# Experts' transposes taken in pairs of blocks, one-hots in the second pair, gathered tokens in one group, and a small tile of norms in another pool

## The chip, the cores and the metric

The kernel runs on one core of a Trainium2 chip. The time is device microseconds of that core, the median of the runs shown.

## What is computed

A decoder trunk of two layers over 256 tokens of width 1024: causal pooling and a dense SwiGLU, then attention over shared keys and values and a layer of eight experts of which each token takes two. The change lies in the experts, whose reference, cut, is:

```python
logits = (xf @ w_router).astype(jnp.float32)
top_val, top_idx = lax.top_k(logits, TOP_K)      # TOP_K = 2
gates = jax.nn.softmax(top_val, axis=-1)
# tokens sorted by expert, each expert's block runs that expert only
h = jax.nn.silu(xb @ w_gate[e]) * (xb @ w_up[e])  # 1024 -> 3584
y_block = h @ w_down[e]                           # 3584 -> 1024
y = jnp.zeros((T, D)).at[tok_s].add(g_s[:, None] * ys[dest])
```

## The kernel before

An expert takes up to 128 tokens at once. Its 3584 inner units are cut into seven blocks of 512 (`hidden_block(b)`, b = 0 to 6). A block is eight steps of gate and up (`ps_mg`, then `ps_mu`), and, from block 2 on, four steps of the down product of the block two before (`ps_y`); the down products of the last two blocks, eight steps, close the expert, so it has 84 steps. A step takes a weight tile of 128x1024 numbers (half of a 1 MB load), splits it into a high part (`wh`, ScalarE, L180) and a low part (`wl`, VectorE, L184), and runs six TensorE matmuls of 512 columns: four with `wh` (L192), two with `wl` (L195). Activations are split the same way (`xeH`/`xeL`, `hid`), so every product is three matmuls.

The order is written by hand. `run()` walks the steps; before a step's matmuls are written down, the splits up to three steps ahead are, and after it `tick()` runs what `later(n, fn)` has put off by n steps. Each engine keeps this order. SyncE fetches weights into a ring of 11 slots of 1 MB, each slot fetched again when its `wl` has been made.

Between the steps TensorE has smaller work, all through the four PSUM banks of `bankB`:

- `turn_hidden(hs, b)`: four transposes of the block's 128x512 inner units (`ps_hT`, L1113), four steps after the block is done; then ScalarE and VectorE write `hid` from PSUM (L1121, L1122). Seven such groups in an expert.
- `seek(e + 1)`, begun six steps into block 2: VectorE writes the next expert's one-hots (L1073); two steps later `find` transposes them (two transposes, L1079), ScalarE copies the result to `ohT` (L1080), and two small products (four passes, L1025) give, in the same PSUM bank, the row numbers of that expert's tokens, which VectorE casts into `src` (L1026); four steps after that GpSimd issues the indirect DMA (L1029) that fetches those rows into `xm`.
- `gather(slots, q, name)`: the fetched tokens are transposed in two groups of four (`ps_x`, L1060) and split into `xeH`/`xeL`; 5 and 8 steps after the last block.
- `scatter`: the expert's output is added to the tokens (L1127 to L1130).

The first expert, expert 0, has more: it takes its tokens by a product (L1064), and the gates of all experts (L987 to L998) and the tokens' store (`ship`, L1011) fall into its first blocks.

`rstds`, 48 numbers per partition of reciprocal norms, lies in the pool `cst`; a filler of 16 numbers lies in `resid`, one of `PHASE_FILL` bytes in `mp`. The pools are laid out one behind the other, so these sizes set the addresses of what follows.

Of the kernel before, what the change touches and what calls it, by code (L numbers as in the profile page):

```python
# [12 lines left out]
F32 = mybir.dt.float32  # L13
# [15 lines left out]
TL = 3  # L29
# [9 lines left out]
TURN = 4  # L39
P = 128  # L40
T = 256
# [4 lines left out]
FE = 3584  # L46
NB = FE // 512
LAG = 2
PHASE_FILL = 160
EPS = 1e-6  # L50
NEG = -1e30
WINDOWS = (2, 4, 8, 16)
# [45 lines left out]
def trunk(ctx, tc, x, a_norm, a_proj, a_scale, kv_norm, w_kv, b_norm, w_q, w_o, rel_bias,  # L98
          ffn_norm, w_gate, w_up, w_down, moe_router, moe_gate, moe_up, moe_down, final_norm,
          c_misc, c_band, c_onehot, c_mask, out):  # L100
    nc = tc.nc
# [5 lines left out]
    cst = ctx.enter_context(tc.tile_pool(name="cst", bufs=1))  # L107
# [4 lines left out]
    resid = ctx.enter_context(tc.tile_pool(name="resid", bufs=1))  # L112
# [23 lines left out]
    def later(n, fn, rank=1):  # L136
        serial[0] += 1
        pending.append((clock[0] + n, rank, serial[0], fn))
# [133 lines left out]
    nc.vector.memset(ones, 1.0)  # L272
    mhalf = cst.tile([P, 2], F32, name="mhalf")
    nc.vector.memset(mhalf, -0.5)
    rstds = cst.tile([P, 48], F32, name="rstds")
    taken = []


# [41 lines left out]
        return ap.rearrange("p (m i r) -> p m i r", i=2, r=2)  # L320

    h2 = resid.tile([P, 2, D], F32, name="h2")
    resid.tile([P, 16], F32, name="fill")
    sq = h2.rearrange("p i (k t) -> p (i k) t", t=T)

    hT_ctx, hp = phase("hp", side="right")
# [483 lines left out]
    mo = {}  # L810
# [5 lines left out]
    def last_merge():  # L816
# [23 lines left out]
        mo["src"] = mp.tile([P, NE], I32, name="src")  # L840
        mp.tile([P, PHASE_FILL // 4], F32, name="fill")
        spare = av["big"][:, 4096:]
# [162 lines left out]
    got = []  # L1005
    rows = dpool.tile([T, D], F32, name="rows")

    def ship():
# [6 lines left out]
        nc.vector.tensor_copy(tok[:, 0:1], pn[:, :1])  # L1015
        nc.vector.tensor_scalar(tok[:, 1:2], pn[:, :1], float(P), None, op0=ALU.add)

    def seek(e):
        plain = plain_onehots(e, mo["pos"], "")

        def find():
            ohT = mo["ohT", e] = mo["m1"].tile([P, 2, P], F32R, tag=f"ohT{e % 2}", name=f"ohT{e}")
            po = turn_onehots(e, plain, ohT, "")
            for i in range(2):
                nc.tensor.matmul(po[:, T:T + 1], plain[:, i, :], mo["tok"][:, i:i + 1], start=(i == 0), stop=(i == 1))  # L1025
            nc.vector.tensor_copy(mo["src"][:, e:e + 1], po[:, T:T + 1])  # L1026

        later(2, find)
        later(6, lambda: nc.gpsimd.indirect_dma_start(  # L1029
            out=mo["xm"][:, e % 2, :], out_offset=None, in_=rows,  # L1030
            in_offset=bass.IndirectOffsetOnAxis(ap=mo["src"][:, e:e + 1], axis=0)))

    then(route)

# [38 lines left out]
            nc.vector.tensor_scalar(plain[:, i, :], iota, slot[:, i, e:e + 1], None, op0=ALU.is_equal)  # L1073
        return plain

    def turn_onehots(e, plain, ohT, sfx):
        po = bankB(f"ps_oh{sfx}{e}")
        for i in range(2):
            nc.tensor.transpose(po[:, i * P:(i + 1) * P], plain[:, i, :], ident)  # L1079
        nc.scalar.activation(ohT.rearrange("p i t -> p (i t)"), po[:, :T], AF.Copy)  # L1080
        return po

# [21 lines left out]
    def expert(e, got, sfx, next_expert=None):  # L1104
# [2 lines left out]
        hidden = [None] * NB  # L1107
        full = (NB - 1,) if next_expert is None else ()

        def turn_hidden(hs, b):  # L1110
            pt = bankB(f"ps_hT{sfx}{e}_{b}")
            for c in range(4):
                nc.tensor.transpose(pt[:, c * P:(c + 1) * P], hs[:, c * P:(c + 1) * P], ident)  # L1113
            ptv = pt.rearrange("p (c s) -> p c s", c=4)
            if b in full:
                hidden[b] = mo["m1"].tile([P, NK, P], F32, tag="xeH", name=f"hid{sfx}{e}_{b}")[:, :4, :]
                nc.scalar.activation(hidden[b], ptv, AF.Copy)
                return
            both = mo["m1"].tile([P, 4, 2, P], F32R, tag="hid", name=f"hid{sfx}{e}_{b}", bufs=3)
            hidden[b] = (both[:, :, 0, :], both[:, :, 1, :])  # L1120
            nc.scalar.activation(hidden[b][0], ptv, AF.Copy)  # L1121
            nc.vector.tensor_sub(hidden[b][1], ptv, hidden[b][0].bitcast(F32))  # L1122
# [13 lines left out]
        def hidden_block(b):  # L1136
            nm = f"{sfx}{e}_{b}"
            ps = {}

            def acc(w):  # L1140
                def f():
                    if w not in ps:
                        ps[w] = bankA(f"ps_m{w}{nm}")
                    return ps[w]
                return f

            def gate_done():
                hs = ps["h"] = mo["m1"].tile([P, 512], F32, tag=f"hs{b % 2}", name=f"hs{nm}")
                nc.scalar.activation(hs, ps["g"], AF.Silu)

            def up_done():
                nc.vector.tensor_mul(ps["h"], ps["h"], ps["u"])
                later(TL if b == NB - 1 and next_expert is None else TURN, lambda: turn_hidden(ps["h"], b))

            for w, src, fn in (("g", moe_gate, gate_done), ("u", moe_up, up_done)):
                for kh in range(2):
                    moe_unit(src[e, kh * 512:(kh + 1) * 512, b * 512:(b + 1) * 512], acc(w),
                             lambda: (got()[1], got()[2]), 4 * kh, kh == 0, kh == 1, f"m{w}{nm}_{kh}",
                             fn if kh == 1 else None)
# [57 lines left out]
    for e in range(NE):  # L1217
        def next_expert(e=e):
            got.append(new_slots(e + 1, ""))
            for q in range(2):  # L1220
                later(5 + 3 * q, lambda q=q: gather(got[e + 1], q, f"{e + 1}_{q}"))

        expert(e, lambda e=e: got[e], "", next_expert if e + 1 < NE else None)
    with tc.manual_schedule():
# [72 lines left out]
```

## Time and profile before

| | us |
|---|---|
| median of 3 runs | 1515.49 (1515.38 to 1523.37) |
| the profiled execution, device time | 1520.44 |
| its span, first to last instruction | 1518.6 |
| TensorE busy in the span | 1488.2 (98%) |
| experts, first step to last product (526.1 to 1505.2) | 979 |

Matmuls are pipelined and the profile models their ends, so they overlap in it: two matmuls of 512 columns that each show 0.39 us start 0.227 us apart. Where TensorE has no gap, the distance from one start to the next is what an instruction costs.

### The profile page before, as it was taken

How to read it: one execution, taken by the hardware profiler on the slowest of the kernel's cores; microseconds unless marked ns; L12 is line 12 of the kernel's file. 1: busy time of each engine (PE TensorE's matmuls, PEld its weight loads, DVE VectorE, ACT ScalarE, POOL GpSimd, SP SyncE). 2: the span in 40 equal slices, each digit the busy share in tenths (PEclk: the TensorE clock that was granted, in tenths of full speed). 3: DMA queues.
4: the chain of work that ended last, by engine and by line, in shares of the span. 5: the costliest groups of instructions: out<-in, count | busy, mean ns of one | idle time of the engine just before them, and what ended most of it. 6: DMA issues, size and time to landing. Idle time of an engine off the chain costs nothing. (4 is left out here: it accounts for less than half of the span.)

```text
span 1518.6 us, 22313 instructions
## 1 busy us (share of the span) xinstructions
PE 1488.2 (98%) x8711; PEld 1300.2 (86%) x8711; DVE 1191.5 (78%) x1341; ACT 1007.2 (66%) x1208; POOL 19.8 (1%) x23
## 2 busy tenths in 40 slices
PE   8999999999999999999999999999999999999996
PEld 7999999999999978888888888888888888888884
DVE  6666556464545588999999899999899899899984
ACT  5444445444444577777777777777777777777773
POOL 0000000000000000000000000000000000000001
PEclk9999999999999999999999999999999999999998
DMA  9955684737464799999999999999999999999931
GB/s 307 313 181 177 192 211 158 201 127 186 139 174 139 281 364 383 374 349 371 366 357 376 376 353 365 378 364 357 370 375 354 374 377 351 368 364 362 371 127 30
DMA packets 276083, 445.79 MB, mean 294 GB/s; under 512 B 28848, under 2 KB 100784, under 8 KB 275968
## 3 DMA queue, kind: packets, MB, share of 16 engines
q1 hardware_dynamic: 252448, 433.11, 80.8%
q10 hardware_dynamic: 22512, 7.50, 3.2%
q0 software_dynamic: 1008, 3.67, 0.6%
q8 instruction: 70, 1.15, 0.3%
q14 instruction: 45, 0.37, 0.1%
HBM read 442.03 MB, written 2.22 MB: 293 GB/s over the span
## 5 line engine op out<-in xcount | busy, mean ns | idle before, releaser
L184 DVE TENSOR_TENSOR wl_mu<-raw_mu,wh_mu 128x1024 fp32r<-128x1024 f32 x196 | 232.1, 1219 | 36.2 <-ACT wh_mu L180 36.2
L184 DVE TENSOR_TENSOR wl_mg<-raw_mg,wh_mg 128x1024 fp32r<-128x1024 f32 x204 | 243.1, 1220 | 15.4 <-ACT wh_mg L180 14.0
L192 PE MATMUL ps_y<-wh_md,hid 128*128 128x512 f32 x880 | 238.2, 392 | 0.0
L180 ACT ACTIVATE wh_mg<-raw_mg 128x1024 fp32r<-128x1024 f32 x204 | 213.5, 1060 | 36.8 <-PE ps_y L192 28.7
L184 DVE TENSOR_TENSOR wl_md<-raw_md,wh_md 128x1024 fp32r<-128x1024 f32 x190 | 223.0, 1219 | 1.5 <-ACT wh_md L180 1.5
L180 ACT ACTIVATE wh_mu<-raw_mu 128x1024 fp32r<-128x1024 f32 x196 | 203.5, 1057 | 20.3 <-PE ps_mg L192 20.2
L180 ACT ACTIVATE wh_md<-raw_md 128x1024 fp32r<-128x1024 f32 x190 | 195.4, 1057 | 22.7 <-PE ps_mu L192 13.6
L192 PEld LDWEIGHTS ps_y<-wh_md,hid 128*128 128x128 f32 x880 | 163.6, 188 | 33.4 <-issue 0.5
L192 PE MATMUL ps_mg<-wh_mg,xeH 128*128 128x512 f32 x448 | 178.6, 399 | 0.0
L192 PE MATMUL ps_mu<-wh_mu,xeH 128*128 128x512 f32 x448 | 176.1, 393 | 0.0
L192 PE MATMUL ps_mg<-wh_mg,xeL 128*128 128x512 f32 x448 | 174.8, 390 | 0.0
L192 PE MATMUL ps_mu<-wh_mu,xeL 128*128 128x512 f32 x448 | 174.5, 389 | 0.0
L195 PE MATMUL ps_mu<-wl_mu,xeH 128*128 128x512 f32 x448 | 138.2, 390 | 1.1 <-DVE wl_mu L184 1.1
L195 PE MATMUL ps_mg<-wl_mg,xeH 128*128 128x512 f32 x448 | 138.3, 390 | 0.0
L195 PE MATMUL ps_y<-wl_md,hid 128*128 128x512 f32 x440 | 135.7, 390 | 0.0
L195 PEld LDWEIGHTS ps_mu<-wl_mu,xeH 128*128 128x128 f32 x448 | 84.0, 188 | 19.3 <-DVE wl_mu L184 1.6
L195 PEld LDWEIGHTS ps_mg<-wl_mg,xeH 128*128 128x128 f32 x448 | 83.9, 188 | 18.5 <-DVE wl_mg L184 0.2
L192 PEld LDWEIGHTS ps_mu<-wh_mu,xeL 128*128 128x128 f32 x448 | 84.2, 188 | 17.0
L192 PEld LDWEIGHTS ps_mu<-wh_mu,xeH 128*128 128x128 f32 x448 | 84.1, 188 | 17.0
L192 PEld LDWEIGHTS ps_mg<-wh_mg,xeL 128*128 128x128 f32 x448 | 84.3, 188 | 16.4
L192 PEld LDWEIGHTS ps_mg<-wh_mg,xeH 128*128 128x128 f32 x448 | 84.2, 188 | 16.3
L195 PEld LDWEIGHTS ps_y<-wl_md,hid 128*128 128x128 f32 x440 | 82.6, 188 | 17.6
(255 smaller groups left out, 2644.5 us busy)
## 6 DMA issues: line engine op xcount, KB each, us to landing
raw_mg<-in_moe_w_gate_dram SPq DMA_DIRECT2D x102, 1024.0 KB, 7.0
raw_mu<-in_moe_w_up_dram SPq DMA_DIRECT2D x98, 1024.0 KB, 7.2
raw_md<-in_moe_w_down_dram SPq DMA_DIRECT2D x96, 1024.0 KB, 6.9
big<-in_moe_w_down_dram SPq DMA_DIRECT2D x16, 1024.0 KB, 7.4
big<-in_moe_w_up_dram SPq DMA_DIRECT2D x14, 1024.0 KB, 6.6
raw_k<-in_w_kv_dram SPq DMA_DIRECT2D x12, 1024.0 KB, 5.3
raw_q<-in_w_q_dram SPq DMA_DIRECT2D x12, 1024.0 KB, 5.5
raw_v<-in_w_kv_dram SPq DMA_DIRECT2D x12, 1024.0 KB, 5.3
```

The costliest lines, as they stand in the source:

```text
L180: nc.scalar.activation(hv, raw, AF.Copy)
L184: nc.vector.tensor_sub(lv, raw, hv.bitcast(F32))
L192: nc.tensor.matmul(o, a, b, start=start and k == 0 and m == 0, stop=False)
L195: nc.tensor.matmul(o, a, b, start=False, stop=stop and k == n - 1)
```

## The change

Three things move and one tile changes its place. Inner units: a done block is put on a list, `waiting`; the list is transposed four steps after blocks 1, 3, 5 and 6, so blocks 0 and 1, 2 and 3, 4 and 5 go together. One-hots: `find` is put on a list, `riders`, which is emptied with the next such group (that of blocks 2 and 3), and its two small products now stand ahead of ScalarE's copy. Tokens: both groups of four are put off by 2 steps. `rstds` goes from `cst` to `resid`, the filler there goes, `PHASE_FILL` is 96: the weight ring, `wh` and `wl` lie 192 bytes lower, the tiles of `xp`, `aqp` and `bigp` 64 lower, those of `mp` and `m1` 64 higher (all shifts are multiples of 64 bytes).

```diff
-PHASE_FILL = 160
+PHASE_FILL = 96
-    rstds = cst.tile([P, 48], F32, name="rstds")
+    rstds = resid.tile([P, 48], F32, name="rstds")
-    resid.tile([P, 16], F32, name="fill")
...
+    riders = []
     def seek(e):
         plain = plain_onehots(e, mo["pos"], "")
         def find():
             ohT = mo["ohT", e] = mo["m1"].tile([P, 2, P], F32R, tag=f"ohT{e % 2}", name=f"ohT{e}")
-            po = turn_onehots(e, plain, ohT, "")
-            for i in range(2):
-                nc.tensor.matmul(po[:, T:T + 1], plain[:, i, :], mo["tok"][:, i:i + 1], start=(i == 0), stop=(i == 1))
+            po = turn_onehots(e, plain, ohT, "", mo["tok"])
             nc.vector.tensor_copy(mo["src"][:, e:e + 1], po[:, T:T + 1])
-        later(2, find)
-        later(6, lambda: nc.gpsimd.indirect_dma_start(
+        riders.append(find)
+        riders.append(lambda: later(3, lambda: nc.gpsimd.indirect_dma_start(
...
+    def turn_onehots(e, plain, ohT, sfx, tok=None):
         po = bankB(f"ps_oh{sfx}{e}")
         for i in range(2):
             nc.tensor.transpose(po[:, i * P:(i + 1) * P], plain[:, i, :], ident)
+        if tok is not None:
+            for i in range(2):
+                nc.tensor.matmul(po[:, T:T + 1], plain[:, i, :], tok[:, i:i + 1], start=(i == 0), stop=(i == 1))
         nc.scalar.activation(ohT.rearrange("p i t -> p (i t)"), po[:, :T], AF.Copy)
...
+        waiting = []
+        def turn_waiting():
+            pts = [(b, turn_hidden(hs, b)) for hs, b in waiting]
+            waiting.clear()
+            while riders:
+                riders.pop(0)()
+            for b, pt in pts:
+                keep_hidden(pt, b)
         def turn_hidden(hs, b):
             pt = bankB(f"ps_hT{sfx}{e}_{b}")
             for c in range(4):
                 nc.tensor.transpose(pt[:, c * P:(c + 1) * P], hs[:, c * P:(c + 1) * P], ident)
+            return pt
+        def keep_hidden(pt, b):
...
-                later(TL if b == NB - 1 and next_expert is None else TURN, lambda: turn_hidden(ps["h"], b))
+                waiting.append((ps["h"], b))
+                if b % 2 or b == NB - 1:
+                    later(TL if b == NB - 1 and next_expert is None else TURN, turn_waiting)
...
-                later(5 + 3 * q, lambda q=q: gather(got[e + 1], q, f"{e + 1}_{q}"))
+                later(2, lambda q=q: gather(got[e + 1], q, f"{e + 1}_{q}"))
```

On TensorE, expert 2, before: the one-hots of expert 3, behind block 2 (its last step's `wl` rows first), with the semaphores that each row waits for.

```order
L195 MATMUL ps_mu_2_8190<-wl_mu_2_1_1_8187,xeH_7812 128x512 [waits DVE_49]
L195 MATMUL ps_mu_2_8190<-wl_mu_2_1_1_8187,xeH_7812 128x512
L1079 MATMUL ps_oh_8234<-misc,oh_8208 128x128 [waits DVE_49] x2
L1025 MATMUL ps_oh_8234<-tok,oh_8208 128x1 [waits Activation_49]
L1025 MATMUL ps_oh_8234<-tok,oh_8208 128x1
L192 MATMUL ps_y_0_8246<-wh_md_0_0_0_8198,hid_0_8081 128x512 x4
```

And in the change, behind the down product of block 1:

```order
L195 MATMUL ps_y_1_8260<-wl_md_1_1_1_8373,hid_1_8180 128x512 [waits DVE_49]
L195 MATMUL ps_y_1_8260<-wl_md_1_1_1_8373,hid_1_8180 128x512
L1125 MATMUL ps_hT_2_8416<-misc,hs_2_8183 128x128 x4
L1125 MATMUL ps_hT_3_8421<-misc,hs_3_8324 128x128 x4
L1078 MATMUL ps_oh_8427<-misc,oh_8207 128x128 [waits PE_49]
L1078 MATMUL ps_oh_8427<-misc,oh_8207 128x128
L1081 MATMUL ps_oh_8427<-tok,oh_8207 128x1 x2
L192 MATMUL ps_mg_4_8444<-wh_mg_4_0_0_8384,xeH_7811 128x512 [waits Activation_49]
```

The small products have lost their wait for ScalarE; the one-hots wait only for TensorE's own earlier use of the bank, blocks 2 and 3 stand together, and the group that stood alone behind block 2 is gone.

On VectorE, expert 0, before, from the last of the gates to the down product of block 0:

```order
L998 SCALAR_TENSOR_TENSOR gat<-sel,gv_5769,gat 128x8
L1122 TENSOR_TENSOR hid_1_6058<-ps_hT_1_6053,hid_1_6058 128x4x128
L184 TENSOR_TENSOR wl_mu_2_1_1_6064<-big_5483,wh_mu_2_1_1_6063 128x1024
L184 TENSOR_TENSOR wl_md_0_0_0_6075<-raw_md_0_0_5550,wh_md_0_0_0_6074 128x1024
L1073 TENSOR_SCALAR oh_6084<-misc,pos 128x128 x2
L184 TENSOR_TENSOR wl_md_0_0_1_6088<-raw_md_0_0_5550,wh_md_0_0_1_6087 128x1024
L184 TENSOR_TENSOR wl_md_1_0_0_6100<-raw_md_1_0_6097,wh_md_1_0_0_6099 128x1024
L1026 CAST src<-ps_oh_6110 128x1
L1152 TENSOR_TENSOR hs_2_6061<-hs_2_6061,ps_mu_2_6067 128x512
L184 TENSOR_TENSOR wl_md_1_0_1_6119<-raw_md_1_0_6097,wh_md_1_0_1_6118 128x1024
```

And in the change:

```order
L997 SCALAR_TENSOR_TENSOR gat<-sel,gv_5768,gat 128x8
L1137 TENSOR_TENSOR hid_0_6054<-ps_hT_0_6044,hid_0_6054 128x4x128
L1137 TENSOR_TENSOR hid_1_6057<-ps_hT_1_6049,hid_1_6057 128x4x128
L184 TENSOR_TENSOR wl_mu_2_1_1_6063<-big_5482,wh_mu_2_1_1_6062 128x1024
L184 TENSOR_TENSOR wl_md_0_0_0_6074<-raw_md_0_0_5549,wh_md_0_0_0_6073 128x1024
L1072 TENSOR_SCALAR oh_6083<-misc,pos 128x128 x2
L184 TENSOR_TENSOR wl_md_0_0_1_6087<-raw_md_0_0_5549,wh_md_0_0_1_6086 128x1024
L184 TENSOR_TENSOR wl_md_1_0_0_6099<-raw_md_1_0_6096,wh_md_1_0_0_6098 128x1024
L1167 TENSOR_TENSOR hs_2_6060<-hs_2_6060,ps_mu_2_6066 128x512
L184 TENSOR_TENSOR wl_md_1_0_1_6110<-raw_md_1_0_6096,wh_md_1_0_1_6109 128x1024
```

`hid_0`, which stood six weight splits earlier, now stands right ahead of `hid_1` and of the last split of block 2; the cast of `src` has gone to the group of blocks 2 and 3.

## Rows read from the trace of the kernel before

**Rows 1.** Page, part 1: busy us, share of the span, instructions.

```profile
PE 1488.2 (98%) x8711; PEld 1300.2 (86%) x8711; DVE 1191.5 (78%) x1341; ACT 1007.2 (66%) x1208; POOL 19.8 (1%) x23
```

**Rows 2.** One expert: stretch, length, busy us by engine, PEclk, DMA share, GB/s.

```profile
782.30:904.20 121.90, 121.43 (x556) 100.28 (x555) 111.52 (x110) 94.93 (x103) 0.94 (x1) 1.00 1.01 367
```

**Rows 3.** Timeline of PE, one group: start, us, line, count [idle before <-releaser].

```profile
602.30 1.07 PE L192 MATMUL ps_y<-wh_md,hid 128*128 128x512 f32 x4
...
603.67 0.60 PE L1113 MATMUL ps_hT<-misc,hs 128*128 128x128 f32 x4
...
606.87 0.39 PE L192 MATMUL ps_mg<-wh_mg,xeH 128*128 128x512 f32 x1
...
608.23 0.39 PE L192 MATMUL ps_mg<-wh_mg,xeH 128*128 128x512 f32 x1
```

**Rows 4.** Timeline of PE, expert 0: two groups that already stand together.

```profile
554.57 0.51 PE L985 MATMUL ps_count<-both,ones 128*128 128x8 f32 x4
554.93 0.63 PE L1113 MATMUL ps_hT<-misc,hs 128*128 128x128 f32 x4
...
559.52 0.39 PE L192 MATMUL ps_mu<-wh_mu,xeH 128*128 128x512 f32 x1
```

**Rows 5.** Timeline of PE, expert 2: the one-hots for expert 3.

```profile
806.93 0.38 PE L1079 MATMUL ps_oh<-misc,oh 128*128 128x128 f32 x2
807.79 0.61 PE L1025 MATMUL ps_oh<-tok,oh 128*128 128x1 f32 x4 [0.47 <-ACT ohT L1080]
808.25 1.17 PE L192 MATMUL ps_y<-wh_md,hid 128*128 128x512 f32 x4
...
811.08 1.07 PE L192 MATMUL ps_y<-wh_md,hid 128*128 128x512 f32 x4
```

**Rows 6.** Waits: engine, line <- waited for: us in total, times, longest.

```profile
PEld ps_oh L1025 <- ACT ohT L1080: 4.9, 7, 0.7
```

**Rows 7.** Timeline of PE, expert 0: the end of block 2 and its one-hots.

```profile
561.72 0.74 PE L195 MATMUL ps_mu<-wl_mu,xeH 128*128 128x512 f32 x2 [1.13 <-DVE wl_mu L184]
563.05 0.52 PE L1079 MATMUL ps_oh<-misc,oh 128*128 128x128 f32 x2 [0.60 <-DVE oh L1073]
...
564.52 1.16 PE L192 MATMUL ps_y<-wh_md,hid 128*128 128x512 f32 x4
```

**Rows 8.** Timeline of DVE in the same place and ahead of it.

```profile
549.86 2.36 DVE L184 TENSOR_TENSOR wl_mg<-raw_mg,wh_mg 128x1024 fp32r<-128x1024 f32 x2 [2.10 <-ACT wh_mg L180]
...
561.58 1.22 DVE L184 TENSOR_TENSOR wl_md<-raw_md,wh_md 128x1024 fp32r<-128x1024 f32 x1
...
563.11 2.35 DVE L184 TENSOR_TENSOR wl_md<-raw_md,wh_md 128x1024 fp32r<-128x1024 f32 x2
...
566.04 1.22 DVE L184 TENSOR_TENSOR wl_md<-raw_md,wh_md 128x1024 fp32r<-128x1024 f32 x1
```

**Rows 9.** Timeline of ACT, expert 0: block 0's `hid`.

```profile
543.19 0.60 ACT L1121 ACTIVATE hid<-ps_hT 128x512 fp32r<-128x512 f32 x1 [1.19 <-PE ps_hT L1113]
543.69 0.59 ACT L1149 ACTIVATE hs<-ps_mg 128x512 f32<-128x512 f32 x1
```

**Rows 10.** Timeline of ACT behind the group of Rows 3.

```profile
604.80 1.05 ACT L180 ACTIVATE wh_mg<-big 128x1024 fp32r<-128x1024 f32 x1
```

**Rows 11.** Timeline of DVE behind the same group.

```profile
605.88 1.23 DVE L184 TENSOR_TENSOR wl_mg<-big,wh_mg 128x1024 fp32r<-128x1024 f32 x1 [0.26 <-ACT wh_mg L180]
```

**Rows 12.** Groups of DVE, 777 to 900 us: busy us, mean ns | idle before.

```profile
L184 DVE TENSOR_TENSOR wl_mu<-raw_mu,wh_mu 128x1024 fp32r<-128x1024 f32 x23 | 27.3, 1217 | 3.3 <-ACT wh_mu L180 3.3
L184 DVE TENSOR_TENSOR wl_mu<-big,wh_mu 128x1024 fp32r<-128x1024 f32 x6 | 7.2, 1220 | 1.6 <-ACT wh_mu L180 1.6
```

**Rows 13.** Timeline of POOL, 800 to 900 us.

```profile
809.07 0.94 POOL L1029 DMA_INDIRECT xm<-rows,src  x1 [120.94 <-DVE src L1026]
```

**Rows 14.** The same line's instructions: time from issue to landing.

```profile
DMA to landing us min/median/max: 5.7/7.9/8.3
```

**Rows 15.** Waits of SyncE's queue.

```profile
SPq L165 <- DVE wl_mg L184: 303.8, 107, 18.8
```

More of the change, by code (lines that the diff above doesn't have):

```diff
@@ L1022, in find @@
             ohT = mo["ohT", e] = mo["m1"].tile([P, 2, P], F32R, tag=f"ohT{e % 2}", name=f"ohT{e}")
-            po = turn_onehots(e, plain, ohT, "")
-            for i in range(2):
-                nc.tensor.matmul(po[:, T:T + 1], plain[:, i, :], mo["tok"][:, i:i + 1], start=(i == 0), stop=(i == 1))
+            po = turn_onehots(e, plain, ohT, "", mo["tok"])
             nc.vector.tensor_copy(mo["src"][:, e:e + 1], po[:, T:T + 1])
-        later(2, find)
-        later(6, lambda: nc.gpsimd.indirect_dma_start(
+        riders.append(find)
+        riders.append(lambda: later(3, lambda: nc.gpsimd.indirect_dma_start(
             out=mo["xm"][:, e % 2, :], out_offset=None, in_=rows,
-            in_offset=bass.IndirectOffsetOnAxis(ap=mo["src"][:, e:e + 1], axis=0)))
+            in_offset=bass.IndirectOffsetOnAxis(ap=mo["src"][:, e:e + 1], axis=0))))
     then(route)
@@ L1074, in plain_onehots @@
         return plain
-    def turn_onehots(e, plain, ohT, sfx):
+    def turn_onehots(e, plain, ohT, sfx, tok=None):
         po = bankB(f"ps_oh{sfx}{e}")
```

## The prediction

> **What bounds the kernel now.** I read the page's busy shares first, then the stretches of single experts, then TensorE's timeline around each small group, and last the waits. TensorE is busy for 98% of the span [rows 1], and in a middle expert for 121.43 of 121.90 us at a granted clock of 1.00, the 2.4 GHz level, while VectorE has 111.52 and ScalarE 94.93 us of work [rows 2]. Busy time alone would not prove a bound, so look at starts: a step of six matmuls follows the last after 1.36 us (606.87 to 608.23 [rows 3]), and 84 such steps are 114.2 of the 121.9 us. The rest is TensorE's small groups, and each moves all that follows by its own length. So in the experts a TensorE wait or switch that goes is time that goes. Weights are not late: SyncE's queue waits for `wl` to free a slot [rows 15], not for memory.
>
> The Trainium skill (Perfetto Trace Analysis, Identifying the Most-Contended Engine) says that matmul busy time is a poor measure of TensorE and that weight-load busy time should be taken. By it TensorE stands at 86% [rows 1] with a seventh of its time to spare, and the sum below would be 0; the even 1.36 us of the steps speaks against that reading here, and it is the third rival below.
>
> **What a switch costs.** From the first of four transposes to the step start two steps behind the next is 606.87 - 603.67 = 3.20 us; two steps are 2.72, so the group costs 0.48. Inside, four take 0.60 us with a last one of 0.27 (their usual length), so one follows the other after 0.11, and four are 0.44 at most (0.435 by finer reading). The switch to transposes and back is therefore about 0.05 [rows 3]. One place shows two groups already together, four count passes and four transposes: from 554.57 to 559.52 are 4.95 us for both and three steps (4.08), so 0.87 [rows 4]; with 0.48 for the transposes the four passes cost 0.39 there, 0.09 less than a group alone. I take 0.05, being the same kind of instruction, and keep 0.03 to 0.09.
>
> *Pairs of blocks.* Three groups fewer in each of eight experts, 24 x 0.05 = 1.2 us. *Tokens in one group:* seven experts, 7 x 0.05 = 0.35. Together 1.55 (0.9 to 2.8), all on TensorE's path.
>
> *One-hots, experts 1 to 6.* The group costs 811.08 - 806.93 - 2.72 = 1.43 us [rows 5], of which most is a stop: the small products wait for ScalarE to copy the transposes out of the bank, 0.7 us seven times [rows 6]. In the change they precede the copy and have no such wait. What is left is two transposes at 0.11 and four passes at (808.25 - 807.79) / 4 = 0.115: 0.68 (0.60 to 0.80), with no switch of its own. Saved 0.75 each, 6 x 0.75 = 4.5 us (3.8 to 5.0).
>
> *One-hots, expert 0.* VectorE is behind here: the last `wl` of block 2 comes 1.13 us late, then the transposes wait 0.60 for VectorE's one-hots, then the products for ScalarE [rows 7]. Block 2 ends at 561.72 + 2 x 0.227 = 562.17; the down product starts at 564.52: 2.35 us, of which 0.68 comes back later, so 1.67. The cover: the down steps now start at 562.17 and ask for their `wl` 0.91 us into each, at 563.08, 564.44, 565.80 and 567.16. VectorE delivers at 562.80 (561.58 + 1.22), 564.33 (563.11 + 1.22), 565.46, and, without the cast of 0.15 ahead of it, 567.11 [rows 8]. All four are in time, the last by 0.05. This is the thinnest cover of the change.
>
> *Block 0's `hid` in expert 0.* It goes from ScalarE's place at 543.19, where ScalarE had waited 1.19 us for the transposes and 0.50 passes before the next instruction starts [rows 9]. ScalarE then waits for the end of `ps_mg` only, about 0.44 earlier, so everything behind is about 0.9 us earlier, and with it the end of VectorE's 2.10 us of idle time at 549.86 [rows 8]. VectorE pays the `hid` back, 0.6 us, ahead of the late `wl`. Net 0.3 us earlier (0 to 0.9), and the four times above move along with it.
>
> *Elsewhere, the joint groups' bursts.* Behind one group `wh` for four steps on is done at 604.80 + 1.05 = 605.85 [rows 10] and wanted at 608.23 [rows 3], 2.38 us ahead; its `wl` is done at 607.11 [rows 11] and wanted at 608.23 + 0.91, 2.03 ahead. With two blocks and the one-hots ScalarE has one more `hid` (0.50) and the `ohT` copy (0.28) to do after the group, so both leads shrink by 0.78, to 1.6 and 1.25. Where the cover ends at zero, none of it costs anything. What queues behind: on ScalarE and VectorE only the next splits.
>
> *The tokens' fetch* is issued 15 steps later (4 steps behind the one-hots at step 8 of block 2, now 3 behind step 24), some 20 us. GpSimd has nothing else; it idled 120.94 us for `src` [rows 13]. The rows land after at most 8.3 us [rows 14], and the first token transposes come 35 steps, 48 us, after the issue. Nothing on SyncE moves. Cost 0.
>
> *Addresses.* The same split reads from the ring and from `big`, which lie 64 bytes apart modulo 256 before the change and after it, in 1217 and 1220 ns [rows 12]: 3 ns x 668 splits (84 an expert, less 4) is 2 us at most, on an engine with 10 us free in each expert [rows 2]. I take 0 and keep 1 us to either side.
>
> Sum: 1.55 + 4.5 + 1.67 + 0.3 = 8.0 us. The profiled execution took 1520.44, so it would take 1512.4; the median lies 4.95 us (0.33%) below it, and what is saved is TensorE's time at full clock in either, so the median goes from 1515.49 to **1507.5**. Bounds: 0.9 + 3.8 + 1.0 = 5.7 (expert 0 with 0.7 lost again) to 2.8 + 5.0 + 2.6 = 10.4.
>
> **The rivals.** *Expert 0 gives it back.* VectorE's chain there has 0.05 us in hand; if its splits or ScalarE's `wh` come a little later than I read them, TensorE waits in the down product of block 0 instead. Then 1.55 + 4.5 + 0.3 are left, 6.4 us: 1509.1. For it: VectorE is busy without a break from 549.86 on; against it: it gains 0.2 us on TensorE with each step that holds no other work.
>
> *Switches cost more.* With 0.09 for each of 31 [rows 4], 1.2 us more goes: 1506.3. Against it: count passes and transposes are different instructions.
>
> *TensorE is not the bound.* VectorE or ScalarE would set the pace, nothing is gained: 1515.5. Against it are leads of 2 us behind every group.
>
> *The wait stays.* Something else in the bank holds the small products; only the joins count: 1513.9.
>
> *Slower: bursts on the path.* Should the leads behind a joint group not be there, since ScalarE now stands still until the whole group is through, each of the 24 groups puts its extra 0.78 us on TensorE: 18.7 - 8.0 = 10.7 us more, 1526.2. It decides from the point at which the lead of 2.03 us is used up, that is if a group costs VectorE 1.25 us more than I count; from 0.33 us of wait for each group on, the whole change loses. Against it: the late `wl` of expert 0 [rows 7] stands behind the gates' arithmetic, which no later expert has.
>
> **How the numbers follow.** About 0.5% is what a measurement of this kernel can tell from no change, here 1507.9. Forecast 0.58 (two thirds of it below 1507.9), expert 0 gives back 0.17, dearer switches 0.14, TensorE not the bound 0.04, the wait stays 0.02, bursts 0.05. Faster: 0.40 + 0.14 = 0.54. Within: 0.18 + 0.17 + 0.04 + 0.02 = 0.41. Slower: 0.05. The range takes in the forecast, expert 0's rival and the dearer switches with the microsecond for addresses: 1504.3 to 1510.7; the three rivals left out hold 0.11.
>
> **What would show it.** In the profile after: no wait of L1081 for ScalarE; joint groups of eight transposes at 0.91 to 0.93 us, of eight with one-hots at 1.6; a middle expert at 121.9 - 0.75 - 4 x 0.05 = 120.95 us; VectorE's leads behind the group of blocks 2 and 3 over 1 us; expert 0's down steps 1.36 us apart. The prediction is wrong if TensorE shows waits for `wl` or `wh` behind the joint groups, if steps far from any group are no longer 1.36 us apart, or if the middle experts are not shorter by 0.9 us.

## The result and the profile after

The changed kernel takes **1501.66 us**, the median of 4 runs (1501.31 to 1503.27). The kernel before, beside it, took 1518.29 (1515.38 to 1523.37, 4 runs), so the ratio is 0.989 with an interval of 0.987 to 0.992. The time lies below the range of 1504.3 to 1510.7.

The executions of the kernel before lie apart by more than those of the changed one. Beside the experiments below its medians were 1521.9 to 1523.5, so the 1515.49 from which the prediction starts was a low sample of three; what lies behind this is taken up below. The two profiled executions can be compared stage by stage: 1520.44 before, 1503.27 after, 17.17 us less. The starts of the experts divide this. Ahead of the first expert 526.12 us became 517.54, **8.58 less**; from the start of the first to the start of the last step of the experts 970.84 became 962.14, **8.70 less**; behind them 0.11 more.

The page, part 1, of the changed kernel, columns as in [rows 1]:

```profile
PE 1476.5 (98%) x8711; PEld 1295.0 (86%) x8711; DVE 1190.2 (79%) x1341; ACT 1011.4 (67%) x1208; POOL 15.4 (1%) x23
```

TensorE has the same 8711 instructions and is busy for 11.7 us less. One middle expert of the changed kernel, columns as in [rows 2]:

```profile
759.75:880.56 120.81, 120.81 (x556) 100.46 (x554) 111.28 (x110) 95.46 (x103) 0.94 (x1) 1.00 1.02 370
```

It takes 120.81 us where 121.90 stood in [rows 2] (121.87 from start to start), and TensorE has no gap left in it: busy time and length are the same.

The groups of the same expert in the timeline of PE, the answers to [rows 3] and [rows 5]: first the pair of blocks 0 and 1, then that of blocks 2 and 3 with the one-hots:

```profile
788.77 1.03 PE L1125 MATMUL ps_hT<-misc,hs 128*128 128x128 f32 x8
789.56 0.48 PE L192 MATMUL ps_mu<-wh_mu,xeH 128*128 128x512 f32 x1
...
792.38 0.39 PE L192 MATMUL ps_mu<-wh_mu,xeH 128*128 128x512 f32 x1
...
816.86 1.03 PE L1125 MATMUL ps_hT<-misc,hs 128*128 128x128 f32 x8
817.73 0.38 PE L1078 MATMUL ps_oh<-misc,oh 128*128 128x128 f32 x2
817.95 0.50 PE L1081 MATMUL ps_oh<-tok,oh 128*128 128x1 f32 x4
818.32 0.48 PE L192 MATMUL ps_mg<-wh_mg,xeH 128*128 128x512 f32 x1
...
821.15 0.39 PE L192 MATMUL ps_mg<-wh_mg,xeH 128*128 128x512 f32 x1
```

Eight transposes cost 792.38 - 788.77 - 2.72 = 0.89 us, with the one-hots 821.15 - 816.86 - 2.72 = 1.57. The difference, 0.68, is what the one-hots cost now; in [rows 5] it was 1.43. The small products follow the transposes without the stop of 0.47.

Two of the waits in the experts of the changed kernel (who waits for whom, us in total, times, longest):

```profile
ACT ohT L1082 <- PE ps_oh L1081: 15.3, 7, 2.2
PE ps_mu L195 <- DVE wl_mu L184: 1.0, 1, 1.0
```

The wait of [rows 6] is gone. In its place ScalarE, which has time, waits longer for TensorE's one-hots: 15.3 us in all, 8.1 before. The one wait of TensorE for a `wl` is that of expert 0, 1.13 us in [rows 7] and 1.0 now.

Expert 0, the end of block 2 in the timeline of PE, which answers to [rows 7]:

```profile
552.80 0.73 PE L195 MATMUL ps_mu<-wl_mu,xeH 128*128 128x512 f32 x2 [1.00 <-DVE wl_mu L184]
553.37 1.09 PE L192 MATMUL ps_y<-wh_md,hid 128*128 128x512 f32 x4
...
554.75 1.08 PE L192 MATMUL ps_y<-wh_md,hid 128*128 128x512 f32 x4
...
556.13 1.07 PE L192 MATMUL ps_y<-wh_md,hid 128*128 128x512 f32 x4
...
557.49 1.07 PE L192 MATMUL ps_y<-wh_md,hid 128*128 128x512 f32 x4
...
558.91 0.39 PE L192 MATMUL ps_mg<-wh_mg,xeH 128*128 128x512 f32 x1
```

The down product starts 0.57 us behind the late `wl_mu`, not 2.80 as before, and its four steps are 1.38, 1.38, 1.36 and 1.42 us long: VectorE's thin cover held.

So the experts did what was forecast. The other half of the gain lies ahead of them, where the order of every engine is the same in both kernels. There TensorE runs matmuls of 256 columns. Here is a stretch of 50 us in the dense layer without any gap, of before and of after (columns as in [rows 2]):

```profile
100.00:150.00 50.00, 50.00 (x427) 50.00 (x426) 33.13 (x36) 22.62 (x28) 0.00 (x0) 1.00 0.49 163
```

```profile
100.00:150.00 50.00, 50.00 (x444) 50.00 (x443) 34.01 (x38) 22.81 (x27) 0.00 (x0) 1.00 0.53 176
```

Both show a TensorE that is busy throughout at a granted clock of 1.00, the 2.4 GHz level; but it does 427 matmuls in the one and 444 in the other (a stretch also counts the two or three that its ends cut). From start to start they are 117.8 ns apart before and 113.3 after.

The whole dense layer and what follows up to the experts (attention and the router), as stretches, of before and of after:

```profile
23.69:215.82 192.13, 190.46 (x1597) 188.27 (x1595) 124.53 (x139) 89.61 (x117) 0.70 (x1) 1.00 0.70 225
215.82:526.12 310.30, 305.12 (x2599) 294.57 (x2597) 168.02 (x285) 147.09 (x239) 1.82 (x3) 1.00 0.61 177
```

```profile
23.23:208.80 185.57, 183.65 (x1597) 181.46 (x1595) 124.36 (x139) 89.57 (x117) 0.70 (x1) 1.00 0.72 234
208.80:517.54 308.74, 304.60 (x2598) 294.33 (x2597) 168.02 (x285) 147.09 (x239) 1.81 (x3) 1.00 0.61 179
```

The same instructions take 6.56 us less in the dense layer and 1.56 less behind it; the remaining 0.46 is an earlier first product. Of the 1.56 only 0.52 is busy time of TensorE (305.12 against 304.60), the rest is idle time.

### The profile page after: what moved, and what is told of

Read it like the earlier page. It is cut to its first block, busy times and chain, and to the rows that moved or that the text cites. A ratio compares the mean times of both kernels' runs of the same rounds, so it can differ in the third digit from the quotient of the medians.

```text
span 1501.5 us, 22339 instructions
## 1 busy us (share of the span) xinstructions
PE 1476.5 (98%) x8711; PEld 1295.0 (86%) x8711; DVE 1190.2 (79%) x1341; ACT 1011.4 (67%) x1208; POOL 15.4 (1%) x23
```

## The experiments

"Distance" is the address of the split activations ahead of the experts minus that of the weight ring, modulo 256 bytes; TensorE reads one as the stationary operand (128 columns) and the other as the moving one (256 columns): in the dense layer and in the products for q the activations move, in those for v the weights do. The distance is 64 before and 192 after the change. In the experts, where the activations are other tiles, it is 0 in both. "Dense" and "attention" are the two stretches above, "ns from start to start" is the mean over the 256-column matmuls of a stage.

| kernel | distance | ns from start to start in dense, q, v | dense, us | attention, us | middle expert, us | median, us | ratio to before |
|---|---|---|---|---|---|---|---|
| before | 64 | 117.8, 117.8, 114.5 | 192.1 | 310.3 | 121.87 | 1518.3 to 1523.5 | 1 |
| after | 192 | 113.4, 115.6, 117.1 | 185.6 | 308.7 | 120.81 | 1501.7 | 0.989 |
| e1 | 192 | 117.8, 115.6, 117.1 | 192.2 | 308.5 | 121.85 | 1515.4 | 0.996 |
| e12, e1 again | 192 | 113.4, 115.6, 117.1 | 185.5 | 310.6 | 121.85 | 1513.5 | 0.994 |
| e2 | 64 | 117.8, 117.8, 114.9 | 192.1 | 314.4 | 120.83 | 1512.6 | 0.994 |
| e3 | 0 | 120.0, 119.9, 119.8 | 195.5 | 312.9 | 121.87 | 1530.6 | 1.006 |
| e4 | 0 | 120.0, 119.9, 119.8 | 195.5 | 313.9 | 122.65 | 1536.3 | 1.011 |
| e13 | 64, shifted | 117.8, 117.8, 114.5 | 192.1 | 310.6 | 121.77 | 1523.5 | 1.001 |
| e14 | 192, shifted | 117.6, 116.7, 117.3 | 192.0 | 309.2 | 120.79 | 1507.2 | 0.990 |
| e5 | 128 | 118.7, 118.7, 118.7 | 193.5 | 312.7 | 120.81 | 1514.9 | 0.996 |
| e6 | 224 | 118.3, 118.3, 117.1 | 193.0 | 309.2 | 120.81 | 1510.7 | 0.992 |

In two of these profiles the granted clock fell to the half in attention, for 3.4 us a time: twice in e2, once in e12. At half clock 3.4 us do the work of 1.7, so without it they would stand at 311.0 and 308.9 us by estimate, near the others of their distance.

The means of q and v hide something. Stream by stream (a stream is a row of at least 20 such matmuls with no other instruction between), before and after run almost every stream either at 113.3 to 114.1 ns or at about 117.8, and the mean tells how many are at which. In v of before four of five streams are at the short spacing, in v of after one of five. In v the operands have changed roles, so counted from the stationary to the moving one its distance is 192 before and 64 after, and it too is mostly short at 192 and mostly long at 64. The trace of before even has the short spacing at its own 64: 3 of the 21 streams of the k product have it. In one of them the first 16 matmuls take 281.62 - 279.81 = 1.81 us, 113.1 ns each:

```profile
279.81 0.28 PE L192 MATMUL ps_k<-akH,wh_k 128*128 128x256 f32 x1
...
281.62 1.07 PE L195 MATMUL ps_k<-akH,wl_k 128*128 128x256 f32 x8
```

**The two halves apart (e1, e2).** e1 is the kernel before with the new addresses:

```diff
-PHASE_FILL = 160
+PHASE_FILL = 96
-    rstds = cst.tile([P, 48], F32, name="rstds")
+    rstds = resid.tile([P, 48], F32, name="rstds")
-    resid.tile([P, 16], F32, name="fill")
```

> The kernel before with the new addresses alone (rstds in resid, the filler there gone, PHASE_FILL 96); the order of every engine is that of before. Theory A, the addresses set the spacing of TensorE's 256-column matmuls: they start 113.3 ns apart in the dense layer as in the changed kernel, the stretch ahead of the experts takes 517.5 us as there and not 526.1, the experts stay at about 970.8 us from first to last step, and the time falls by 8.6 us, a ratio of 0.994. Theory B, the spacing differs from execution to execution whatever the addresses: no fixed change, ratio 1.000 within 0.3%, the stretch is 526 or 517 by chance. Theory C, the addresses act in the experts too, through the 512-column matmuls behind a group: the experts take 0.2 to 0.5 us each less, and the time falls by 10 to 12 us.

Its ratio was 0.9961 (0.9943 to 0.9979), and the experts stayed at 121.85 us. The addresses alone are worth 6 us here, 9 in e12 below. But this one profiled execution showed 117.8 ns in the dense layer, not 113.3, while the attention layer had the changed kernel's spacings. It was the longest of ten executions, 1520.95; the other nine took 1512.6 to 1517.5. Neither A nor B explains both.

e2 is the changed kernel with these three edits undone.

> The changed kernel with the addresses of before: joint groups, one-hots and token groups as changed, rstds, filler and PHASE_FILL as they were. Theory A: the stretch ahead of the experts takes 526.1 us again, with 117.8 ns between the matmuls of the dense layer; the experts take 962.1 us, as changed; the time is 8 to 8.7 us below before, a ratio of 0.9945. Theory B: the stretch is 526 or 517 by chance, the ratio anywhere from 0.989 to 0.995. Theory C: the experts take 963 to 965 us and the ratio is about 0.996.

The ratio was 0.9942 (0.9920 to 0.9964), the experts took 962.27 us from first to last step and the spacings ahead of them were those of before. The stretch ahead of them took 532.19 us and not 526.1, with the two falls of the clock in attention and a first product of the dense layer 1.9 us later. So the order is worth 8.6 us at either addresses (970.84 - 962.27 here, 970.72 - 962.14 from e12 to the changed kernel), which is theory A; the product of the two ratios, 0.990, is the whole change within the intervals. C fell: the experts do not care.

**Which operand (e3, e4).** e3 drops only the filler, e4 only moves `rstds`:

```diff
-    resid.tile([P, 16], F32, name="fill")
```

> The kernel before without the filler in resid alone: the split activations of the layers ahead of the experts (the moving operand of the 256-column matmuls in the dense layer, k and q) lie 64 bytes lower, 224 modulo 256 as in the changed kernel; the weight ring with wh and wl stays at 224. The rest stays where it was. If the moving operand's address decides: 113.3 ns in the dense layer, the stretch ahead of the experts at 517.5 us, ratio 0.994. If the ring's address decides, or the distance of the two matters and equal phases are slow: 117.8 ns and 526.1 us, ratio 1.000. Theory B: no fixed change. The experts are as before in each.

```diff
-    rstds = cst.tile([P, 48], F32, name="rstds")
+    rstds = resid.tile([P, 48], F32, name="rstds")
```

> The kernel before with rstds moved to resid alone: the weight ring, wh and wl lie 192 bytes lower, 32 modulo 256 as in the changed kernel; the split activations ahead of the experts stay at 32, those of the experts at 224. If the ring's address decides (stationary operand ahead of the experts): 113.3 ns in the dense layer and 517.5 us, ratio 0.994. If the moving operand's decides: 117.8 ns and 526.1 us, ratio 1.000. In the experts the ring is the moving operand and differs in its phase from the stationary one here, which it does in neither kernel: if the distance of the two matters, their steps are no longer 1.36 us apart in the settled stretches, and each expert is longer or shorter by up to 4%, 5 us. Theory B: no fixed change.

Neither operand decides by itself: each half of the move made things worse, 1.0064 (1.0043 to 1.0085) and 1.0105 (1.0070 to 1.0141). With both at the same address modulo 256 the 256-column matmuls settle at 120.0 ns from start to start, which was none of the values expected. The stretch of the dense layer in e3 (columns as above):

```profile
100.00:150.00 50.00, 50.00 (x419) 50.00 (x418) 32.90 (x36) 22.76 (x27) 0.00 (x0) 1.00 0.54 174
```

In the experts, with 512 columns, it is the other way round: e4 is the only kernel in which the ring and the experts' operands lie 64 bytes apart, and there the settled steps go round between 226, 229 and 232 ns a matmul where all others show 226.7, and an expert is 0.78 us longer. The output product of attention (`ps_o`), 512 columns with the weights moving, has other distances: over its starts that lie 215 to 245 ns apart the mean is 228.3 ns at equal addresses (e3, e4), 229.3 after, 232.4 in e5, 233.1 in e6 and 233.3 before.

**Distance or place (e13, e14).** Both operands moved together, by 64 bytes down from before and up from after:

```diff
-PHASE_FILL = 160
+PHASE_FILL = 224
-    rstds = cst.tile([P, 48], F32, name="rstds")
+    rstds = cst.tile([P, 32], F32, name="rstds")
```

> The kernel before with everything that TensorE reads moved down by 64 bytes together (rstds of 32 numbers, PHASE_FILL 224): ring 160, activations ahead of the experts 224, experts 160 modulo 256. The distances are those of before, the activations stand where those of the changed kernel stand. If the distance of the two operands decides: as before, 117.8 ns in the dense layer, k and q at 117 to 117.8, v at 114.5, ratio 1.000. If a place decides: like the changed kernel's addresses, 113.3 ns in the dense layer, v at 117.1, ratio 0.994.

```diff
-PHASE_FILL = 96
+PHASE_FILL = 32
     rstds = resid.tile([P, 48], F32, name="rstds")
+    cst.tile([P, 16], F32, name="fill")
```

> The changed kernel with the same moved up by 64 bytes together (a filler of 16 numbers in cst, PHASE_FILL 32): ring 96, activations ahead of the experts 32, as in the kernel before, experts 96 modulo 256; the distances are the changed kernel's. If the distance decides: 113.3 ns in the dense layer, v at 117.1, the stretch ahead of the experts 517.5 to 519 us, the experts 962.1, ratio 0.988. If a place decides: 117.8 ns, v at 114.5, the stretch at 526 us, ratio 0.993.

e13 repeats before in every spacing, ratio 1.0008 (0.9991 to 1.0025): the place is not what decides. e14 has attention spacings close to the changed kernel's, but its profiled execution, against what was expected of the distance, ran the dense layer at 117.8 ns from its second block on and took 1509.25; two of its other three took 1504.99 and 1505.08, one 1512.24. With the changed kernel's distance the dense layer can therefore run at either level, as in e1.

**What chooses between the two levels (e7, e8, e11, e12).** e8 is the changed kernel once more, e12 is e1 once more.

> The changed kernel once more, beside other kernels. Theory L, with unequal addresses of the two operands the 256-column matmuls run at 113.3 or 117.8 ns, chosen where TensorE's stream starts again after a gap and held until the next gap: the dense layer shows one of the two levels through and through, 113.3 more often than not; an execution with 117.8 takes 6.7 us longer, so the times lie in two groups, about 1501.5 and 1508, and the median is 1501 to 1503. Theory P, each pair of addresses has its own fixed level and e1's profile differs for another reason: 113.3 ns and one group of times.

> The kernel before with the new addresses alone, once more. Its profiled execution on record was the longest of ten (1520.95 us, 117.8 ns in the dense layer), the other nine took 1512.6 to 1517.5. Theory L: most executions run the dense layer at 113.3 ns, so this profile most likely shows it, with a stretch ahead of the experts of 517.5 to 518.5 us and an execution of 1512 to 1514; if it is 117.8 again, 524.5 and 1519 or more. If the order of the experts, too, decides the level ahead of them (it can't by the instructions, which are the same up to there): 117.8 in every execution, and the shorter times are the clock's.

e8: 113.3 ns again, 1503.63 us (1501.22 to 1504.31), ratio 0.9873 (0.9847 to 0.9899), one group of times, so these four executions do not tell L from P. e12: 113.3 ns this time, 185.5 us for the dense layer instead of 192.2, 518.34 us to the first expert instead of 524.71, ratio 0.9938 (0.9922 to 0.9955). The same program at the same addresses runs its dense layer at one level in one execution and at the other in the next. Of the seven profiled executions at a distance of 192 whose dense layer was left alone (after, e1, e8, e9, e10, e12, e14), five ran at 113.3; of the three at 64 (before, e2, e13), none.

e7 puts transposes that nobody reads between the units of the dense layer (a unit is the gate or the up product of one block), `kick("g")` and `kick("u")` behind each from block 2 on:

```diff
+        def kick(nm):
+            if b > 1:
+                pk = bankB(f"ps_kick{nm}{b}")
+                for c in range(1 + b % 3):
+                    nc.tensor.transpose(pk[:, c * P:(c + 1) * P], ident, ident)
...
```

> The changed kernel with 1, 2 or 3 transposes put between the units of the dense layer (18 places, from its third block on), which write a bank that nobody reads. Theory L: each place chooses the level anew, so both 113.3 and 117.8 ns stand in the dense layer of this one execution, each held from one place to the next. Theory P: 113.3 ns between all of them. The transposes themselves cost about 0.11 us each and 0.04 to 0.09 a place, 36 x 0.11 + 18 x 0.06, some 5 us in all; the experts take 962.1 us.

Both levels stood in one execution: at all 12 places with one or three transposes the following unit ran at 113.5 ns, at all 6 places with two at 117.8 (behind the last of them it is the whole down product), each held to the next place. Timeline of PE in e7, the start of two units, behind two transposes and behind three; then the two units as stretches:

```profile
85.85 0.38 PE L515 MATMUL ps_kicku<-misc 128*128 128x128 f32 x2
85.98 0.36 PE L192 MATMUL ps_g<-xfH,wh_g 128*128 128x256 f32 x1
86.19 0.28 PE L192 MATMUL ps_g<-xfL,wh_g 128*128 128x256 f32 x1
...
91.73 0.49 PE L515 MATMUL ps_kickg<-misc 128*128 128x128 f32 x3
91.97 0.37 PE L192 MATMUL ps_u<-xfH,wh_u 128*128 128x256 f32 x1
92.18 0.28 PE L192 MATMUL ps_u<-xfL,wh_u 128*128 128x256 f32 x1
```

```profile
86.00:91.80 5.80, 5.80 (x52) 5.80 (x50) 4.44 (x5) 2.53 (x3) 0.00 (x0) 1.00 0.60 179
92.10:97.60 5.50, 5.50 (x51) 5.50 (x50) 2.88 (x3) 2.53 (x3) 0.00 (x0) 1.00 0.55 191
```

The level is chosen where the stream of equal matmuls starts again, and stays until the next interruption. With the 36 transposes, and five units and the whole down product at 117.8, the dense layer took 193.0 us, and the ratio was 0.9949 (0.9932 to 0.9967). e11 puts the same transposes into the kernel before:

> The kernel before, its addresses too, with the same 1, 2 or 3 transposes at the 18 places of the dense layer. In the changed kernel 1 and 3 led to 113.5 ns and 2 to 117.9 at each place. Theory L: here too both levels stand in the one dense layer, each held to the next place and set by the number of transposes, with the same or the opposite assignment. If the addresses of before allow 117.8 alone: 117.8 at all places, and what the changed kernel gained in the dense layer is its addresses'.

There 17 of 18 places led to 117.8 ns and one to 113.4; the ratio was 1.0025 (1.0010 to 1.0040), the transposes for nothing. So the distance of before allows the short spacing too, but leads to it rarely, and the number of transposes alone does not set the level: the one place had three, like five others that led to 117.8.

**Other distances (e5, e6).** e5 shortens `rstds` in the changed kernel, e6 adds a filler:

```diff
-    rstds = resid.tile([P, 48], F32, name="rstds")
+    rstds = resid.tile([P, 32], F32, name="rstds")
```

> The changed kernel with rstds of 32 instead of 48 numbers (18 are used), so that the split activations ahead of the experts lie at 160 modulo 256, 128 away from the ring at 32; the experts' tiles stay. Theory L: unequal addresses, so 113.3 or 117.8 ns, drawn anew after each gap; the stretch ahead of the experts is 517 to 524 us. Theory P: a level of its own, unknown, the same in the whole dense layer and in k, q and v wherever the distance is the same, since 128 is 128 in either direction: v and q show the same spacing, where they differed at a distance of 64 (117.1 against 116.3 ns). The experts take 962.1 us.

```diff
     h2 = resid.tile([P, 2, D], F32, name="h2")
+    resid.tile([P, 8], F32, name="fill")
```

> The changed kernel with a filler of 8 numbers in resid: the split activations ahead of the experts lie at 0 modulo 256 instead of 224, the ring stays at 32, so the distance is 32 and no multiple of 64. If only equal addresses modulo 256 are held back: 113.3 or 117.8 ns, the stretch at 517 to 524 us. If what counts is that both lie in the same 64 bytes: 120.0 ns as with equal addresses, and 531 us or more. The experts take 962.1 us.

e5 has one level everywhere, 118.7 ns, as theory P said and L did not; e6 has 118.3, and 117.1 in v, which neither of its two expectations said. Ratios 0.9961 (0.9941 to 0.9980) and 0.9921 (0.9896 to 0.9947), with the changed order in both. Two levels to choose from were seen at 64 and 192 only; none of the tried distances beats 192.

**The terms of the sum (e9, e10).** e9 is the changed kernel with the old one-hots, e10 is e1 with the small products ahead of the copy and nothing joined:

```diff
-            po = turn_onehots(e, plain, ohT, "", mo["tok"])
+            po = turn_onehots(e, plain, ohT, "")
+            for i in range(2):
+                nc.tensor.matmul(po[:, T:T + 1], plain[:, i, :], mo["tok"][:, i:i + 1], start=(i == 0), stop=(i == 1))
...
-        riders.append(find)
...
+        later(2, find)
...
```

> The changed kernel with the one-hots put back (their own group two steps after it is asked for, small products behind ScalarE's copy, rows fetched four steps later); pairs of blocks and the joint token groups stay. If a join saves 0.05 us, as predicted: a middle expert takes 121.85 - 4 x 0.05 = 121.65 us. If it saves what the groups of the changed kernel show, 0.081 for each pair and 0.074 for the tokens: 121.85 - 0.32 = 121.53. The stretch ahead of the experts is as in the changed kernel, 517.5 to 519, or 6.7 more if the dense layer runs at 117.8 ns.

```diff
-            po = turn_onehots(e, plain, ohT, "")
-            for i in range(2):
-                nc.tensor.matmul(po[:, T:T + 1], plain[:, i, :], mo["tok"][:, i:i + 1], start=(i == 0), stop=(i == 1))
+            po = turn_onehots(e, plain, ohT, "", mo["tok"])
...
```

> The kernel before with the new addresses (as in the run with these alone) and one edit of the order: the two small products of the one-hots stand ahead of ScalarE's copy. No group is joined. If TensorE's stop for the copy is what the one-hots cost: a middle expert falls by 0.70 us (1.43 - 0.68 - 0.05 for the switch that stays), from 121.85 to 121.15, and the trace shows no wait of the small products for ScalarE. If the stop only covers another wait (VectorE's or ScalarE's splits being late behind it): under 0.2 us an expert. Expert 0 falls by 0.5 only, as its transposes still wait 0.6 us for VectorE's one-hots.

e9: 121.57 us for a middle expert, 0.28 for four joins, so **0.07 a join**, ratio 0.9924 (0.9907 to 0.9940). e10: 121.11, so the stop for ScalarE's copy is worth **0.74**, ratio 0.9907 (0.9891 to 0.9924). Its one-hots in the timeline of PE:

```profile
797.75 0.38 PE L1076 MATMUL ps_oh<-misc,oh 128*128 128x128 f32 x2
797.97 0.50 PE L1079 MATMUL ps_oh<-tok,oh 128*128 128x1 f32 x4
798.34 1.17 PE L192 MATMUL ps_y<-wh_md,hid 128*128 128x512 f32 x4
...
801.17 1.07 PE L192 MATMUL ps_y<-wh_md,hid 128*128 128x512 f32 x4
```

801.17 - 797.75 - 2.72 = 0.70 us for the group that took 1.43 in [rows 5], though it still stands alone: joined to the pair it costs 0.68, so here the switch is worth 0.02 and not 0.07. The parts add up: 121.85 - 0.28 - 0.74 = 120.83, and 120.81 was measured.

## Why the prediction was wrong, point by point

*The failed step is "Addresses".* It looked at the one engine for which the trace of before had a pair of addresses to compare, VectorE's splits [rows 12], found 3 ns there, and took 0, keeping 1 us. The engine that bounds the kernel reads the same moved tiles, and for it no row of before showed two distances for one stage. The 1 us was thus no bound on TensorE. A bound was in reach: the trace of before has 256-column matmuls at 117.8 ns in the dense layer and at 114.5 in v, the same shape with the roles of the two operands exchanged, and 3.3 ns on the dense layer's 1584 matmuls are 5.2 us. What the runs showed in its place: 6.6 us in the dense layer, in the executions in which it runs at 113.3 ns, and 1.6 in attention (1.8 in e1). Of the latter the changed means of q (2.2 ns shorter on 576 matmuls), k, v and o explain about 0.8. Most of the rest is a shorter wait of TensorE for ScalarE's split of the k weights, in the waits of the attention stretch of before and of the changed kernel:

```profile
PE ps_k L192 <- ACT wh_k L180: 3.9, 4, 1.3
PE ps_k L192 <- ACT wh_k L180: 3.0, 4, 1.2
```

The other profiles at 192 show 2.6 to 4.2 us of this wait, so that this part is the change's doing is not shown.

*The base.* "What is saved is TensorE's time at full clock in either, so the median goes from 1515.49": the saving in the experts is the same in either, but the 4.95 us between profile and median were not noise around one kernel. An execution whose dense layer runs at 113.3 ns is 6.6 us shorter, and two of the three runs shown were probably such. The later times of before bear this out. Taken at the same mean granted clock they stand in two groups: at 0.994 five from 1515.76 to 1517.81 and nine from 1521.28 to 1523.37, at 0.993 five from 1517.67 to 1518.96 and fifteen from 1521.71 to 1525.66, the groups 5.7 to 5.8 us apart in the mean. No profile of an execution of the lower group exists, so it stays an inference that the dense layer makes the difference. The low base also made the miss look smaller, by luck: from the later medians of before, 1521.9 to 1523.5, the same 8.0 us would have led to 1513.9 to 1515.5, twelve to fourteen above what was measured, where the forecast stands 5.8 above it.

*The range.* Its own bounds, 5.7 to 10.4 saved with 1 us for addresses to either side, give 1504.1 to 1510.8 and not 1504.3 to 1510.7; the time lies below both.

*A switch, 0.05 us (0.03 to 0.09).* The rival "switches cost more" was nearer: 0.07 by e9, in the middle of the bounds. Thirty-one of them are 2.2 us, not 1.55.

*One-hots, experts 1 to 6, 0.75 each.* Right: e9 to after is 121.57 - 120.81 = 0.76, the stop alone 0.74 by e10, what is left 0.68 as worked out.

*Expert 0, 1.67 + 0.3.* From its start to the next 123.37 became 121.40, 1.97 with its four joins in it, so about 1.7 where 1.97 was forecast beside the joins: the 0.3 for `hid` does not show. The four down steps came in time; "expert 0 gives it back" did not happen. e10 takes away one of its three stops, that for the copy, and shows 122.67, 0.75 under e12's 123.42, where 0.5 was expected; the changed kernel takes away that for VectorE's one-hots too, since they are asked for with the pair.

*Tokens' fetch, SyncE, bursts: 0.* Right: up to the last step of the experts TensorE has no wait but the one shown.

*Sum.* 8.0 forecast in the experts, 8.7 measured; middle experts 120.95 forecast, 120.81 measured; joint groups 0.91 to 0.93 and 1.6 against 0.89 and 1.57.

*TensorE is not the bound.* This rival rested on weight-load busy time, 86% before and 86% after. The Trainium skill (Perfetto Trace Analysis, Identifying the Most-Contended Engine) would have TensorE's headroom judged by it, or by the share of peak arithmetic; here the stop taken from TensorE in e10 came off the time in full (0.74, forecast 0.70), so in this kernel the even starts were the better evidence.

*"Steps far from any group are no longer 1.36 us apart"* was named as what would prove the prediction wrong. It watched the 512-column steps of the experts, which stayed at 1.36; the 256-column ones ahead of them were not watched.

## What to carry to other kernels

When an edit moves tiles, ask of each engine which pair of operands it streams at once, and of the bounding engine first; an address that costs one engine nothing says nothing of another. Count instructions in equal stretches without gaps: a busy share of 100% at full clock hid 4%. And where executions of one program differ by a fixed amount, find the stage that differs before taking a median as the base.

## What the runs showed of the hardware that I had not expected

**The spacing of fp32r matmuls depends on where the two operands lie to each other.** 256 columns: 113.3 ns at best, 117.8, 118.3, 118.7 or 120.0 else, at a granted clock of 1.00 in the stretches of 50 us compared. 512 columns: 226.7 when settled with equal addresses modulo 256, 229 with 64 bytes between (e4). Of the distances tried, equal addresses are the worst for 256 columns (e3, e4) and the best for 512 (also in `ps_o`). What in the chip does this was not tried.

The Trainium skill (SBUF — State Buffer, A bandwidth-pool intuition that's wrong) gives TensorE an independent second read port for loading weights. If that were all, e3 and e4 would hardly differ from before. The measurement decides: where the two operands lie to each other changes TensorE's pace (117.8 against 120.0 ns), by whatever way. The gap that the Trainium skill states for a single warm matmul (TensorE: Matmul & The Clock Gate, Back-to-back issue gap) is 262 cycles at 256 columns, an estimated 109.2 ns at 2.4 GHz. No settled stream here is below 113 ns.

**Two levels with memory.** At 64 and 192 bytes a stream takes one of two spacings when it starts and keeps it until it is interrupted, 100 us and more in the dense layer. In e7 one transpose more or fewer in the interruption told the level at all 18 places; in e11, at the other distance, it did not. What decides at the dense layer's own interruptions stays open.

**In expert 0 the clock fell only where its three stops stood.** Stretch of e9, the first steps of the down product in expert 0 (PEclk is the third number from the end):

```profile
557.83:561.24 3.41, 3.41 (x10) 2.58 (x10) 2.85 (x3) 1.57 (x2) 1.18 (x1) 0.53 1.06 398
```

The granted clock is close to the 1.2 GHz level there. Just before, TensorE had stopped three times, by the waits of e9 from 540 to 570 us:

```profile
PE ps_mu L195 <- DVE wl_mu L184: 1.0, 1, 1.0
PE ps_oh L1080 <- DVE oh L1074: 0.7, 1, 0.7
PE ps_oh L1026 <- ACT ohT L1084: 0.5, 1, 0.5
```

Expert 0 takes 1.6 us longer in such an execution (124.98 in e1, 123.42 in e12). It was so in four of the eight profiles whose expert 0 has all three stops (e1, e3, e9, e11), and in none of the eight in which it has one or two (after, e2, e5, e6, e7, e8, e10, e14). That the changed order spares the kernel this is likely, and would be part of its gain over the medians of before, but it rests on these sixteen profiles alone and no run tried it.
